# Nine chunks of a down projection as two-by-two blocks with seven products

## The chip, the cores and the metric

One core of a Trainium2 chip runs the kernel alone. The engines are TensorE (PE, whose weight loads the profile shows apart as PEld), VectorE (DVE), ScalarE (ACT), GpSimd (POOL) and SyncE (SP, which issues the transfers). The metric is the device time of one execution in microseconds; lower is better.

## The reference

Two layers, 256 tokens of 1024 features, all float32. Each layer is a half-step FFN, an attention mixer, and another half-step FFN. The change lies in the FFNs:

```python
def swiglu(h, w_gate, w_up, w_down):
    return (jax.nn.silu(h @ w_gate) * (h @ w_up)) @ w_down

for i in range(DEPTH):
    h = rmsnorm(x, ffn1_norm[i])
    x = x + 0.5 * swiglu(h, ffn1_w_gate[i], ffn1_w_up[i], ffn1_w_down[i])
    ...                         # the mixer adds to x
    h = rmsnorm(x, ffn2_norm[i])
    x = x + 0.5 * swiglu(h, ffn2_w_gate[i], ffn2_w_up[i], ffn2_w_down[i])
```

`w_gate` and `w_up` are 1024 x 2816, `w_down` is 2816 x 1024. The four FFNs are named here by (layer, which of the two): (0,1), (0,2), (1,1), (1,2).

## The kernel before

**Numbers in two parts.** TensorE multiplies in a reduced float32 form (F32R). Every operand is therefore held as `hi` (a cast of the float32 value, on ACT) and `lo` (value minus `hi`, on DVE), and each product is three matmuls: hi·hi, hi·lo and lo·hi. `dense` issues these three (lines L379, L382, L385), each with a stationary operand of 128 x 128 and 512 moving columns into one PSUM bank.

**Weights in chunks.** The weights pass through in chunks of 128 x 2048 floats (1 MB). `loader` issues a chunk's transfers on SP into one of three `raw` buffers (L270); `split_hi` casts it in four pieces of 512 columns on ACT (L300), `split_lo` subtracts in four pieces on DVE (L310). The pairs of hi and lo have four buffers (`NHL`). A chunk gives its pair back after its last use on TensorE, its `raw` buffer after its last `lo`.

**An FFN** has two stages. In the gate-and-up stage 11 groups of 256 hidden columns are computed, two chunks each, for two blocks `tb` of 128 tokens, into banks `gu`. `evac` forms h = silu(gate)·up (ACT `sil`, DVE `h`), turns it through DRAM (`hb`, `hd`, `hr`; transfers on SP) and splits it into `ht` (hi on ACT L515, lo on DVE L517). In the down stage 11 chunks of `w_down`, each two k-rows of 128 by two column halves `hf` of 512, are multiplied with `ht` into four banks `acc[tb][hf]`: 8 products, 24 matmuls a chunk. Chunks 0 to 7 go one after the other; the last three are the tail, in which the order is by (tb, hf) and then by chunk, so that one bank after the other is finished. `finish` then does x += 0.5·acc on DVE (L462), and `prep_half` transposes that half of x on TensorE (`xtp`, L392) and splits it for the next stage.

**What sets the order.** The program is laid out by a small planner (`Flow`): generators yield conditions or times, and an instruction is emitted when its modelled time has come. Each engine then runs its instructions in that order and waits on semaphores. The planner emits a split when a buffer pair is free in its model (`hl_left`), and, unless the chunk is due, only when its model of the engine is nearly free.

The chunks are numbered through the program: (0,2) has down chunks 73 to 83, (1,1) 106 to 116, (1,2) 153 to 163. So `lo79` is the lo part of down chunk 6 of (0,2).

Of the kernel before, what the change touches and what calls it, by code (L numbers as in the profile page):

```python
# [12 lines left out]
F32 = mybir.dt.float32  # L13
F32R = mybir.dt.float32r
# [28 lines left out]
SLACK = 0.4  # L43
AHEAD = 0
# [98 lines left out]
def kernel(  # L143
# [10 lines left out]
    nc = tc.nc  # L154
    PSUM = bass.MemoryType.PSUM
    NRAW, NHL, NT2 = 3, 4, 19
    flow = Flow()
# [3 lines left out]
    whl = ctx.enter_context(tc.tile_pool(name="whl", bufs=NHL))  # L161
# [15 lines left out]
    def bank(name, shape=(P, 4, P)):  # L177
        return banks.take(list(shape), F32, name)
# [61 lines left out]
    class Chunk:  # L240
        def __init__(self, parts):
            self.parts = parts
            self.raw = self.hi = self.lo = None
            self.arrive = self.early = None
            self.hit = [None] * 4
            self.lot = [None] * 4
            self.uses = 0

    chunks = []
    raw_left = [NRAW]  # L250
# [3 lines left out]
    at = [0]  # L254

    def add_chunk(parts, uses=8):
        c = Chunk(parts)
        c.uses = uses
        c.index = len(chunks)
        chunks.append(c)  # L260
        return c

    def loader():
        for i, c in enumerate(chunks):
            yield lambda: raw_left[0] > 0
            raw_left[0] -= 1
            c.raw = wraw.tile([P, 2048], F32, tag="raw", name=f"raw{i}")
            dma_free[0] = max(dma_free[0], flow.now)
            for j, (dst, src) in enumerate(c.parts):
                nc.sync.dma_start(out=dst(c.raw), in_=src)  # L270
                dma_free[0] += 2.9 / len(c.parts)
                if j == 1 and i < 2:
                    c.early = dma_free[0] + LAT
                    if i:
                        load_x(1, 1)
                        dma_free[0] += 0.7
            c.arrive = dma_free[0] + LAT
            if i == 0:
                load_x(1, 0)
                load_x(0, 1)  # L280
                dma_free[0] += 1.4
            if i > 4 and late_done[0] < len(late_loads):
                dst, src = late_loads[late_done[0]]
                late_done[0] += 1
                nc.sync.dma_start(out=dst, in_=src)
                dma_free[0] += 0.3

    def split_hi():
        for i, c in enumerate(chunks):
            yield lambda: c.raw is not None and hl_left[0] > 0  # L290
            hl_left[0] -= 1
            yield c.early or c.arrive
            c.hi = whl.tile([P, 2048], F32R, tag="hi", name=f"hi{i}")
            c.lo = whl.tile([P, 2048], F32R, tag="lo", name=f"lo{i}")
            for q in range(4):
                if q == 2:
                    yield c.arrive
                yield lambda: flow.free["A"] <= flow.now + SLACK or i <= at[0] + AHEAD
                sl = slice(q * 512, (q + 1) * 512)
                nc.scalar.copy(out=c.hi[:, sl], in_=c.raw[:, sl])  # L300
                c.hit[q] = flow.act(512)

    def split_lo():
        for i, c in enumerate(chunks):
            for q in range(4):
                yield lambda: c.hit[q] is not None
                yield c.hit[q]
                yield lambda: flow.free["V"] <= flow.now + SLACK or i <= at[0] + AHEAD
                sl = slice(q * 512, (q + 1) * 512)
                nc.vector.tensor_sub(c.lo[:, sl], c.raw[:, sl], c.hi.bitcast(F32)[:, sl])  # L310
                c.lot[q] = flow.dve(512)
            raw_left[0] += 1

    def k4(t):
        return t.rearrange("p (k n) -> p k n", k=4)
# [1 line left out]
    def k2(t):  # L317
        return t.rearrange("p (k n) -> p k n", k=2)
# [6 lines left out]

    def rows2(w, r):
        return [(lambda raw: k2(raw), w[r * 256:(r + 1) * 256, :].rearrange("(k p) n -> p k n", p=P))]

    def turned2(w, r):
        src = w[r * 256:(r + 1) * 256, :].rearrange("(k b i) n -> b i k n", k=2, b=4)  # L330
        return [((lambda raw, b=b: k2(raw)[b::4]), src[b]) for b in range(4)]
# [6 lines left out]
    def plan_ffn(l, nm, wg, wu, wd):  # L338
        gu = []
        for g in range(NG):  # L340
            ids = []
            for c in range(2):
                pieces = 2 if len(chunks) < 2 else 1
                a = cols4(wg[l], c, g * 256, 256, 0, pieces)
                b = cols4(wu[l], c, g * 256, 256, 256, pieces)
                ids.append(add_chunk([q for ab in zip(a, b) for q in ab]))
            gu.append(ids)
        plan[l, nm, "gu"] = gu
        dn = []
        for c in range(NG):  # L350
            dn.append(add_chunk(turned2(wd[l], c)))
        plan[l, nm, "dn"] = dn

    for l in range(DEPTH):
# [17 lines left out]
    def dense(ps, xh, xl, ready, c, need, sl, start, stop):  # L372

        flow.until(lambda: c.lot[need] is not None and ready() is not None)
        flow.at(ready())
        flow.at(c.lot[need])
        at[0] = max(at[0], c.index)
        wh, wl = sl(c.hi), sl(c.lo)
        nc.tensor.matmul(out=ps, lhsT=xh, rhs=wh, start=start, stop=False)  # L379
        flow.pe(T_MM)  # L380
        flow.step()
        nc.tensor.matmul(out=ps, lhsT=xh, rhs=wl, start=False, stop=False)  # L382
        flow.pe(T_MM)
        flow.step()
        nc.tensor.matmul(out=ps, lhsT=xl, rhs=wh, start=False, stop=stop)  # L385
        c.uses -= 1
        if c.uses == 0:
            hl_left[0] += 1
        return flow.pe(T_MM)

    def turn(dst, src, flipped=False):
# [82 lines left out]
    def ffn(l, nm, xt, gc_next):  # L474
        hts = [None] * NG
        htt = [None] * NG

        def evac(g, ps, end):
# [41 lines left out]
            hts[g], htt[g] = ht, t  # L520

        for g, ids in enumerate(plan[l, nm, "gu"]):
            flow.until(banks.has(2))
# [23 lines left out]

        SPLIT = NG - 3
        for c in range(SPLIT):
            for k in range(2):  # L550
                for tb in range(2):
                    for hf in range(2):
                        down(c, k, tb, hf)
            g4.give()
            if (l, nm) == (0, 1) and c == 2:
                flow.spawn(memory_prep())
# [814 lines left out]
```

## Time and profile before

| | |
|---|---|
| median of 3 runs | 970.88 us (970.84 to 972.41) |
| the profiled execution | 970.84 us, span from first to last instruction 969.1 us |
| TensorE matmuls | 960.4 us busy, 4552 instructions |
| VectorE | 681.8 us, 1428 instructions |
| ScalarE | 545.7 us, 1167 instructions |
| GpSimd | 60.2 us, 65 instructions |
| moved by transfers | 204.03 MB, 211 GB/s on average |

A share of busy time is a mean over all stages. What limits a stage is read from that stage: who waits there, and for whom. The durations of matmuls in the profile overlap, so their price is the distance from one start to the next.

### The profile page before, as it was taken

The numbers are of one execution on the slowest core, as the hardware profiler recorded it, in microseconds if no ns is written. First come the engines' busy times: TensorE is split into PE (matmuls) and PEld (weight loads), VectorE is DVE, ScalarE is ACT, GpSimd is POOL, SyncE is SP. The second block draws the span as 40 slices with busy tenths as digits, with TensorE's granted clock in tenths as the row PEclk, the third lists the DMA queues.
The fourth block names the chain that finished last, engine by engine and source line by source line (L and its number), as shares of the span: only waits on it lengthen the run. The fifth ranks groups of instructions, "written<-read, shape, count | busy, mean of one in ns | idle before, by whom it ended". The sixth has DMA issues, their size and how long they took to land.

```text
span 969.1 us, 13332 instructions
## 1 busy us (share of the span) xinstructions
PE 960.4 (99%) x4552; PEld 788.3 (81%) x4552; DVE 681.8 (70%) x1428; ACT 545.7 (56%) x1167; POOL 60.2 (6%) x65
## 2 busy tenths in 40 slices
PE   8999999999999999999999999999999999999998
PEld 7888888888777888888888888888787788888886
DVE  6777777788787877665566666654999986666641
ACT  6665555667675655554455545443677764545440
POOL 0000000021210000000000000000344100000000
PEclk9999999999999999999999999999999999999999
DMA  9988877385525587776648777764641468877741
GB/s 286 323 272 279 262 261 242 128 283 195 175 90 171 182 254 238 237 248 231 197 132 275 245 228 247 239 218 132 211 137 50 139 199 265 252 249 240 236 131 43
DMA packets 169295, 204.03 MB, mean 211 GB/s; under 512 B 9674, under 2 KB 144395, under 8 KB 169227
## 3 DMA queue, kind: packets, MB, share of 16 engines
q1 hardware_dynamic: 169226, 203.18, 65.3%
q8 instruction: 35, 0.57, 0.2%
q14 instruction: 34, 0.27, 0.1%
HBM read 188.99 MB, written 14.16 MB: 210 GB/s over the span
## 4 chain that ended last, share of the span: by engine, by line
PE 93%; DVE 4%; ACT 1%; DMA 1%; SPq 0%; issue 0%; ACTq 0%
PE gu L385 16%; PE gu L382 16%; PE gu L379 16%; PE acc L379 10%; PE acc L385 10%; PE acc L382 10%; PE pj L385 3%; PE pj L382 3%; PE pj L379 3%; DVE lo L310 1%; PE xtp L392 1%; PE S L1012 1%; PE AV L1093 1%; PE ptp L392 1%; PE kv L382 1%; PE kv L385 1%
## 5 line engine op out<-in xcount | busy, mean ns | idle before, releaser
L310 DVE TENSOR_TENSOR lo<-raw,hi 128x512 fp32r<-128x512 f32 x656 | 418.0, 684 | 196.2 <-ACT hi L300 182.6
L300 ACT CAST hi<-raw 128x512 fp32r<-128x512 f32 x656 | 367.0, 618 | 281.0 <-PE gu L385 149.9
L385 PE MATMUL gu<-hi,xl 128*128 128x512 f32 x704 | 274.3, 390 | 0.0
L379 PE MATMUL gu<-hi,xh 128*128 128x512 f32 x704 | 274.1, 389 | 0.0
L382 PE MATMUL gu<-lo,xh 128*128 128x512 f32 x704 | 274.0, 389 | 0.0
L382 PEld LDWEIGHTS gu<-lo,xh 128*128 128x128 f32 x704 | 132.2, 188 | 27.4
L385 PEld LDWEIGHTS gu<-hi,xl 128*128 128x128 f32 x704 | 132.2, 188 | 27.3
L379 PEld LDWEIGHTS gu<-hi,xh 128*128 128x128 f32 x704 | 132.2, 188 | 27.3
L379 PE MATMUL acc<-hi,ht 128*128 128x512 f32 x352 | 137.6, 391 | 0.0
L382 PE MATMUL acc<-lo,ht 128*128 128x512 f32 x352 | 137.2, 390 | 0.0
L385 PE MATMUL acc<-hi,ht 128*128 128x512 f32 x352 | 137.1, 390 | 0.0
L385 PEld LDWEIGHTS acc<-hi,ht 128*128 128x128 f32 x352 | 66.1, 188 | 13.7
L382 PEld LDWEIGHTS acc<-lo,ht 128*128 128x128 f32 x352 | 66.1, 188 | 13.5
L379 PEld LDWEIGHTS acc<-hi,ht 128*128 128x128 f32 x352 | 66.1, 188 | 13.5
L385 PE MATMUL pj<-hi,xl 128*128 128x512 f32 x160 | 64.5, 403 | 0.0
L382 PE MATMUL pj<-lo,xh 128*128 128x512 f32 x160 | 63.6, 397 | 0.0
L379 PE MATMUL pj<-hi,xh 128*128 128x512 f32 x160 | 63.5, 397 | 0.0
L487 ACT ACTIVATE sil<-gu,xr 128x256 f32<-128x256 f32 x88 | 41.4, 471 | 22.6 <-PE gu L385 22.6
L490 DVE SCALAR_TENSOR_TENSOR h<-gu,xr,sil 128x256 f32<-128x256 f32 x88 | 42.3, 480 | 2.3
L399 POOL TENSOR_TENSOR xr<-v,nhalf 128x1 f32<-128x1 f32 x12 | 8.4, 697 | 506.3 <-DVE v L397 506.3
L517 DVE TENSOR_TENSOR ht<-hr,ht 128x512 fp32r<-128x512 f32 x44 | 30.2, 686 | 13.4 <-ACT ht L515 12.9
L498 DVE STREAM_TRANSPOSE hb<-h 128x256 f32<-128x256 f32 x88 | 38.7, 440 | 1.1
(165 smaller groups left out, 828.0 us busy)
## 6 DMA issues: line engine op xcount, KB each, us to landing
raw<-in_ffn_w_down_dram SPq DMA_DIRECT2D x176, 256.0 KB, 4.1
raw<-in_ffn_w_gate_dram SPq DMA_DIRECT2D x86, 512.0 KB, 4.1
raw<-in_ffn_w_up_dram SPq DMA_DIRECT2D x86, 512.0 KB, 5.1
raw<-in_w_in_dram SPq DMA_DIRECT2D x32, 512.0 KB, 4.9
hd<-hb SPq DMA_DIRECT2D x44, 256.0 KB, 2.0
hr<-hd SPq DMA_DIRECT2D x44, 256.0 KB, 5.2
raw<-in_w_out_dram SPq DMA_DIRECT2D x8, 1024.0 KB, 4.9
raw<-in_w_mem_kv_dram SPq DMA_DIRECT2D x4, 1024.0 KB, 5.4
```

Of the source, the lines that this page charges most:

```text
L300: nc.scalar.copy(out=c.hi[:, sl], in_=c.raw[:, sl])
L310: nc.vector.tensor_sub(c.lo[:, sl], c.raw[:, sl], c.hi.bitcast(F32)[:, sl])
L379: nc.tensor.matmul(out=ps, lhsT=xh, rhs=wh, start=start, stop=False)
L382: nc.tensor.matmul(out=ps, lhsT=xh, rhs=wl, start=False, stop=False)
L385: nc.tensor.matmul(out=ps, lhsT=xl, rhs=wh, start=False, stop=stop)
L392: nc.tensor.transpose(out=dst, in_=src, identity=flip if flipped else ident)
L487: nc.scalar.activation(sil, ps[tb][:, 0:256], AF.Silu, scale=xt.r[tb])
L490: nc.vector.scalar_tensor_tensor(out=h, in0=ps[tb][:, 256:512], scalar=xt.r[tb], in1=sil, op0=ALU.mult, op1=ALU.mult)
L498: nc.vector.transpose(out=hb[:, :, tb].rearrange("p b f j -> p f b j"), in_=h.rearrange("p (f b i) -> p f b i", f=2, b=4))
L517: nc.vector.tensor_sub(lo, src, hi.bitcast(F32))
L1012: nc.tensor.matmul(out=ss[e][:, pr, :nk], lhsT=q[rows, pr, :], rhs=k[rows, pr, :], start=i == 0, stop=i == len(passes) - 1)
L1093: nc.tensor.matmul(out=av[64 * e:64 * e + 64, pr, :], lhsT=vsrc(kb, pr, e), rhs=pts[e][:, pr, kb, :], start=(kb == 0), stop=(kb == nb - 1))
```

## The change

In (0,2) and (1,1) down chunks 1, 4 and 6, and in (1,2) down chunks 1, 4 and 7, are computed as a product of two-by-two blocks. The blocks of h are (tb, k), those of the weights (k, hf). Seven block products take the place of eight (Strassen's scheme in Winograd's form):

- The weights need four sums of blocks (`wsum`, DVE, float32), and seven blocks are split into hi and lo where four were. Such a chunk takes two of the four buffer pairs.
- h needs four sums of its blocks (`sf`, 128 x 128 each, DVE); seven blocks of h are split (`h7`, in place of `ht`).
- Three of the seven products go into banks of `acc`. The other four are summed over the stage's three such chunks in four banks of their own (`m1`, `m5`, `m6`, `m7`).
- After the last of the three, `seven_sums` copies m1 to SBUF (ACT) and adds it and the other banks to x: four additions (L611) and four updates of x (L606) on DVE.

The core of the diff:

```diff
+    SEVEN = {(0, 1): (), (0, 2): (1, 4, 6), (1, 1): (1, 4, 6), (1, 2): (1, 4, 7)}
...
     def split_hi():
         for i, c in enumerate(chunks):
-            yield lambda: c.raw is not None and hl_left[0] > 0
-            hl_left[0] -= 1
+            n = 2 if c.seven else 1
+            yield lambda: c.raw is not None and hl_left[0] >= n
+            hl_left[0] -= n
...
     def split_lo():
         for i, c in enumerate(chunks):
-            for q in range(4):
+            if c.seven:
+                yield lambda: c.hi is not None and g2.left >= 6
+                yield c.arrive
+                r = [c.raw[:, q * 512:(q + 1) * 512] for q in range(4)]
+                t = [g2.take([P, 512], F32, "wsum") for _ in range(4)]
+                c.block = lambda q, r=r, t=t: ([r[0], r[2], r[3]] + t)[q]
+                for j, x, y in ((0, r[1], r[0]), (1, r[3], t[0]), (2, r[3], r[1]), (3, r[2], t[1])):
+                    yield calm_v(i)
+                    nc.vector.tensor_sub(t[j], x, y)
+                    c.tt[j] = flow.dve(512)
+            for q in range(7 if c.seven else 4):
...
+        def seven_forms(g, src):
+            yield lambda: g4.left >= 2 and g2.left >= 4 and (sv.index(g) < 2 or prog[0] >= sv[1])
+            ht = [g4.take([P, 8, P], F32R, "h7") for _ in range(2)]
+            sf = g2.take([P, 4, P], F32, "sf")
+            s1, s2, s3, s4 = (sf[:, j].rearrange("p (a j) -> p a j", a=4) for j in range(4))
+            for op, o, x, y in ((nc.vector.tensor_add, s1, src[:, 2], src[:, 3]), (nc.vector.tensor_sub, s2, s1, src[:, 0]),
+                                (nc.vector.tensor_sub, s3, src[:, 0], src[:, 2]), (nc.vector.tensor_sub, s4, src[:, 1], s2)):
+                op(o, x, y)
...
+        def seven(c, ms):
+            flow.until(lambda: hts[c] is not None)
+            ht, first, last = hts[c], c == sv[0], c == sv[-1]
+            for q, j, m in ((0, 0, 0), (1, 1, None), (2, 6, None), (3, 3, 1), (4, 4, 2), (5, 5, 3), (6, 2, None)):
+                ps = ms[m] if m is not None else acc.ps[q // 6][q // 2 % 2 if q < 6 else 0]
+                t = dense(ps, ht[0][:, j], ht[1][:, j], lambda: htt[c], dn[c], q, None,
+                          first and m is not None, last and m is not None)
...
+        def seven_sums(ms, t):
+            def into_x(tb, hf, v):
+                sl = slice(hf * 512, (hf + 1) * 512)
+                nc.vector.scalar_tensor_tensor(out=xs[tb][:, sl], in0=v, scalar=0.5, in1=xs[tb][:, sl],
+                                               op0=ALU.mult, op1=ALU.add)
...
+            nc.scalar.copy(out=u, in_=ms[0])
...
+            into_x(0, 0, u)
+            yield plus(u, u, ms[2])
+            plus(w, u, ms[1])
+            into_x(0, 1, w)
+            yield plus(u, u, ms[3])
+            into_x(1, 0, u)
+            yield plus(u, u, ms[1])
+            into_x(1, 1, u)
...
         for c in range(SPLIT):
+            prog[0] = c
+            if c in sv:
+                if c == sv[0]:
+                    flow.until(banks.has(4))
+                    ms = [bank(f"m{j}", (P, 512)) for j in (1, 5, 6, 7)]
+                t = seven(c, ms)
+                if c == sv[-1]:
+                    flow.spawn(seven_sums(ms, t))
+                continue
```

Two places where instructions move. First, VectorE ahead of the tail of (0,2). There, before, stand the lo's of chunks 9 and 10 (`lo82`, `lo83`), that of the next FFN's first chunk (`lo84`), and then x and its preparation:

```order
L310 TENSOR_TENSOR lo81_4683<-raw81_4590,hi81_4682 128x512 x4
L310 TENSOR_TENSOR lo82_4720<-raw82_4626,hi82_4719 128x512 x4
L310 TENSOR_TENSOR lo83_4757<-raw83_4665,hi83_4756 128x512 x4
L310 TENSOR_TENSOR lo84_4794<-raw84_4704,hi84_4793 128x512 x4
L462 SCALAR_TENSOR_TENSOR x0_85<-acc00_4463,x0_85 128x512
```

And now, from the same lo of chunk 9 to the third lo of chunk 10 (`msum` are the sums u and w, `m5` to `m7` the banks):

```order
L340 TENSOR_TENSOR lo82_0_4812<-raw82_4756,hi82_0_4811 128x512
L606 SCALAR_TENSOR_TENSOR x0_85<-msum_4818,x0_85 128x512
L611 TENSOR_TENSOR msum_4818<-msum_4818,m6_4544 128x512
L340 TENSOR_TENSOR lo82_0_4812<-raw82_4756,hi82_0_4811 128x512
L611 TENSOR_TENSOR msum_4819<-msum_4818,m5_4543 128x512
L606 SCALAR_TENSOR_TENSOR x0_85<-msum_4819,x0_85 128x512
L611 TENSOR_TENSOR msum_4818<-msum_4818,m7_4545 128x512
L340 TENSOR_TENSOR lo82_0_4812<-raw82_4756,hi82_0_4811 128x512
L606 SCALAR_TENSOR_TENSOR x1_86<-msum_4818,x1_86 128x512
L340 TENSOR_TENSOR lo82_0_4812<-raw82_4756,hi82_0_4811 128x512
L611 TENSOR_TENSOR msum_4818<-msum_4818,m5_4543 128x512
L340 TENSOR_TENSOR lo83_0_4843<-raw83_4797,hi83_0_4842 128x512
```

Behind these stand the last update of x from `msum`, three lo's of chunk 10, two of `lo84`, and x from `acc00`. The eight operations of `seven_sums` have come between the lo's of chunks 9 and 10.

Second, VectorE ahead of down chunk 6 of (0,2), whose lo's are `lo79`. Before:

```order
L310 TENSOR_TENSOR lo78_4563<-raw78_4437,hi78_4562 128x512 x2
L517 TENSOR_TENSOR ht_4569<-hr_4537,ht_4569 128x512
L310 TENSOR_TENSOR lo78_4563<-raw78_4437,hi78_4562 128x512 x2
L310 TENSOR_TENSOR lo79_4605<-raw79_4510,hi79_4604 128x512 x4
L310 TENSOR_TENSOR lo80_4644<-raw80_4545,hi80_4643 128x512 x4
```

And now (the rows named `sf` and `h7` are the forms of h for this chunk):

```order
L340 TENSOR_TENSOR lo78_0_4638<-raw78_4534,hi78_0_4637 128x512 x4
L573 TENSOR_TENSOR sf_4680<-hr_4157 128x128
L573 TENSOR_TENSOR sf_4680<-sf_4680,hr_4157 128x128
L573 TENSOR_TENSOR sf_4680<-hr_4157 128x128
L573 TENSOR_TENSOR sf_4680<-hr_4157,sf_4680 128x128
L586 TENSOR_TENSOR h7_4679<-hr_4157,h7_4678 128x256
L586 TENSOR_TENSOR h7_4679<-hr_4157,h7_4678 128x128
L586 TENSOR_TENSOR h7_4679<-sf_4680,h7_4678 128x512
L334 TENSOR_TENSOR wsum_4717<-raw79_4567 128x512
L334 TENSOR_TENSOR wsum_4718<-raw79_4567,wsum_4717 128x512
L334 TENSOR_TENSOR wsum_4719<-raw79_4567 128x512
L334 TENSOR_TENSOR wsum_4720<-raw79_4567,wsum_4718 128x512
```

Seven lo's of chunk 6 follow where four stood, and the last `ht` (that of chunk 10) has moved ahead, between the lo's of chunk 4.

More of the change, by code (lines that the diff above doesn't have):

```diff
@@ L244, in __init__, with part @@
             self.arrive = self.early = None
-            self.hit = [None] * 4
-            self.lot = [None] * 4
+            self.seven = False
+            self.hit = [None] * 7
+            self.lot = [None] * 7
+            self.tt = [None] * 4
             self.uses = 0
+        def part(self, lo, q):
+            t = (self.lo if lo else self.hi)
+            if self.seven:
+                t, q = t[q // 4], q % 4
+            return t[:, q * 512:(q + 1) * 512]
     chunks = []
@@ L267, in loader @@
             c.raw = wraw.tile([P, 2048], F32, tag="raw", name=f"raw{i}")
+            c.block = lambda q, c=c: c.raw[:, q * 512:(q + 1) * 512] if not c.seven else c.raw[:, (0, 2, 3)[q] * 512:
+                                                                                          (1, 3, 4)[q] * 512]
             dma_free[0] = max(dma_free[0], flow.now)
@@ L286, in loader, with calm_a, calm_v @@
                 dma_free[0] += 0.3
+    def calm_a(i):
+        return lambda: flow.free["A"] <= flow.now + SLACK or i <= at[0] + AHEAD
+    def calm_v(i):
+        return lambda: flow.free["V"] <= flow.now + SLACK or i <= at[0] + AHEAD
     def split_hi():
         for i, c in enumerate(chunks):
-            yield lambda: c.raw is not None and hl_left[0] > 0
-            hl_left[0] -= 1
+            n = 2 if c.seven else 1
+            yield lambda: c.raw is not None and hl_left[0] >= n
+            hl_left[0] -= n
             yield c.early or c.arrive
-            c.hi = whl.tile([P, 2048], F32R, tag="hi", name=f"hi{i}")
-            c.lo = whl.tile([P, 2048], F32R, tag="lo", name=f"lo{i}")
-            for q in range(4):
+            c.hi, c.lo = ([whl.tile([P, 2048], F32R, tag=x, name=f"{x}{i}_{j}") for j in range(n)] for x in ("hi", "lo"))
+            if not c.seven:
+                c.hi, c.lo = c.hi[0], c.lo[0]
+            for q in range(7 if c.seven else 4):
                 if q == 2:
                     yield c.arrive
-                yield lambda: flow.free["A"] <= flow.now + SLACK or i <= at[0] + AHEAD
-                sl = slice(q * 512, (q + 1) * 512)
-                nc.scalar.copy(out=c.hi[:, sl], in_=c.raw[:, sl])
+                if c.seven and q >= 3:
+                    yield lambda: c.tt[q - 3] is not None
+                    yield c.tt[q - 3]
+                yield calm_a(i)
+                nc.scalar.copy(out=c.part(0, q), in_=c.block(q))
                 c.hit[q] = flow.act(512)
@@ L304, in split_lo @@
         for i, c in enumerate(chunks):
-            for q in range(4):
+            if c.seven:
[8 more added lines that the diff above has]
+                    c.tt[j] = flow.dve(512)
+            for q in range(7 if c.seven else 4):
                 yield lambda: c.hit[q] is not None
                 yield c.hit[q]
-                yield lambda: flow.free["V"] <= flow.now + SLACK or i <= at[0] + AHEAD
-                sl = slice(q * 512, (q + 1) * 512)
-                nc.vector.tensor_sub(c.lo[:, sl], c.raw[:, sl], c.hi.bitcast(F32)[:, sl])
+                yield calm_v(i)
+                nc.vector.tensor_sub(c.part(1, q), c.block(q), c.part(0, q).bitcast(F32))
                 c.lot[q] = flow.dve(512)
-            raw_left[0] += 1
+                if q == 3:
+                    raw_left[0] += 1
+            if c.seven:
+                g2.give(4)
     def k4(t):
@@ L351, in plan_ffn @@
             dn.append(add_chunk(turned2(wd[l], c)))
+            if c in SEVEN[l, nm]:
+                dn[-1].seven, dn[-1].uses = True, 7
         plan[l, nm, "dn"] = dn
@@ L377, in dense @@
         at[0] = max(at[0], c.index)
-        wh, wl = sl(c.hi), sl(c.lo)
+        wh, wl = (c.part(0, need), c.part(1, need)) if sl is None else (sl(c.hi), sl(c.lo))
         nc.tensor.matmul(out=ps, lhsT=xh, rhs=wh, start=start, stop=False)
@@ L387, in dense @@
         if c.uses == 0:
-            hl_left[0] += 1
+            hl_left[0] += 2 if c.seven else 1
         return flow.pe(T_MM)
@@ L476, in ffn @@
         htt = [None] * NG
+        sv = SEVEN[l, nm]
+        prog = [-1]
         def evac(g, ps, end):
@@ L510, in evac @@
             yield flow.now + 4.0
+            src = hr.rearrange("p a (c j) -> p c a j", c=4)
+            if g in sv:
+                yield from seven_forms(g, src)
+                return
             yield g4.has()
             ht = g4.take([P, 2, 4, P], F32R, "ht")
-            src = hr.rearrange("p a (c j) -> p c a j", c=4)
             hi, lo = (ht[:, i].rearrange("p c (a j) -> p c a j", a=4) for i in range(2))
@@ L520, in evac @@
             hts[g], htt[g] = ht, t
+        def seven_forms(g, src):
[6 more added lines that the diff above has]
+                op(o, x, y)
+                t = flow.dve(P, 0.06)
+            yield t
+            view = lambda x: x.rearrange("p c (a j) -> p c a j", a=4)
+            parts = ((slice(0, 2), src[:, 0:2], view(ht[0][:, 0:2]), view(ht[1][:, 0:2])),
+                     (slice(2, 3), src[:, 3:4], view(ht[0][:, 2:3]), view(ht[1][:, 2:3])),
+                     (slice(3, 7), sf, ht[0][:, 3:7], ht[1][:, 3:7]))
+            ts = []
+            for js, x, hi, lo in parts:
+                nc.scalar.copy(out=hi, in_=x)
+                ts.append(flow.act(P * (js.stop - js.start)))
+            for (js, x, hi, lo), t in zip(parts, ts):
+                yield t
+                nc.vector.tensor_sub(lo, x, hi.bitcast(F32))
+                t = flow.dve(P * (js.stop - js.start))
+            g2.give(2)
+            hts[g], htt[g] = ht, t
@@ new lines, in seven @@
+        def seven(c, ms):
[5 more added lines that the diff above has]
+                          first and m is not None, last and m is not None)
+            g4.give(2)
+            return t
@@ new lines, in seven_sums, with plus @@
+        def seven_sums(ms, t):
[3 more added lines that the diff above has]
+                                               op0=ALU.mult, op1=ALU.add)
+                flow.dve(512)
+            def plus(o, v, m):
+                nc.vector.tensor_add(o, v, m)
+                return flow.dve(512)
+            yield t
+            yield g2.has(2)
+            u, w = (g2.take([P, 512], F32, "msum") for _ in range(2))
+            nc.scalar.copy(out=u, in_=ms[0])
+            yield flow.act(512)
+            banks.give()
+            calm = lambda: flow.free["V"] <= flow.now + SLACK
+            yield calm
+            into_x(0, 0, u)
+            yield calm
+            yield plus(u, u, ms[2])
+            banks.give()
+            yield calm
+            plus(w, u, ms[1])
+            into_x(0, 1, w)
+            yield calm
+            yield plus(u, u, ms[3])
+            banks.give()
+            yield calm
+            into_x(1, 0, u)
+            yield calm
+            yield plus(u, u, ms[1])
+            banks.give()
+            into_x(1, 1, u)
+            g2.give(2)
```

## The prediction

> **What bounds the kernel now.** I read the page first (engines, chain), then TensorE's waits, then the three down stages that the change touches, then single instructions in them. The page:
>
> ```profile
> span 969.1 us, 13332 instructions
> PE 960.4 (99%) x4552; PEld 788.3 (81%) x4552; DVE 681.8 (70%) x1428; ACT 545.7 (56%) x1167; POOL 60.2 (6%) x65
> PE 93%; DVE 4%; ACT 1%; DMA 1%; SPq 0%; issue 0%; ACTq 0%
> ```
>
> TensorE is the bound: 99% busy, 93% of the chain. Its waits in the whole run, longest first, begin with the start of the program and then fall to single waits of 0.4 us:
>
> ```profile
> PE xtp L392 <- DMA x<-in_x_dram: 1.6, 1, 1.6
> PE warm L1298 <- POOL ident masks.py:199: 1.3, 1, 1.3
> PE acc L379 <- DVE oT L1000: 0.4, 1, 0.4
> ```
>
> None is in a down stage of an FFN. The three down stages in question (layer 0 FFN 2, layer 1 FFN 1, layer 1 FFN 2), busy time by engine:
>
> ```profile
> 437.50:497.30 59.80, 59.80 (x271) 49.52 (x270) 30.54 (x51) 25.06 (x48) 0.55 (x1) 1.00 0.57 185
> 618.70:678.60 59.90, 59.90 (x271) 49.60 (x270) 30.37 (x51) 26.63 (x50) 0.55 (x1) 1.00 0.58 189
> 905.20:965.20 60.00, 60.00 (x265) 49.38 (x263) 24.08 (x39) 18.99 (x35) 0.00 (x0) 1.00 0.39 128
> ```
>
> PE is full, DVE half busy (behind the length and PE and PE's loads: 30.54 of 59.80 us), ACT 42%, the DMA engines 57%, the clock 1.00. So a matmul taken out here shortens the stage as long as the splits on ACT and DVE keep ahead. The price of a matmul is its distance to the next. First and last of the 264 in the last down stage:
>
> ```profile
> 905.21 0.39 PE L379 MATMUL acc<-hi,ht 128*128 128x512 f32 x1
> ...
> 964.82 0.39 PE L385 MATMUL acc<-hi,ht 128*128 128x512 f32 x1
> ```
>
> (964.82 − 905.21) / 263 = 0.2267 us (0.39 is a duration that overlaps its neighbours). A chunk of 24 takes 5.44 us. The Trainium skill (TensorE: Matmul & The Clock Gate, Part 1) gives 215.7 ns start to start at 512 columns; this trace has 226.7, and the trace decides; by the page the saving below would be an estimated 5.8 us.
>
> How the splits follow TensorE:
>
> ```profile
> 442.72 0.39 PE L385 MATMUL acc<-hi,ht 128*128 128x512 f32 x1
> 443.15 2.18 ACT L300 CAST hi<-raw 128x512 fp32r<-128x512 f32 x4 [2.38 <-PE acc L385]
> 443.80 2.50 DVE L310 TENSOR_TENSOR lo<-raw,hi 128x512 fp32r<-128x512 f32 x4 [1.62 <-ACT hi L300]
> 465.56 2.50 DVE L310 TENSOR_TENSOR lo<-raw,hi 128x512 fp32r<-128x512 f32 x4 [2.94 <-ACT hi L300]
> ```
>
> A chunk's last matmul slot ends at 442.95 (442.72 + 0.23); 0.20 us later ACT starts the hi casts into the freed buffer, and 0.65 us after that DVE starts the lo's. Four lo's last 2.50 us, so with 0.684 for one they start 0.605 apart; ACT's four last 2.18, so 0.52 apart. In every 5.44 us cycle DVE then idles 2.94. The chunk split here is read by PE three chunks (16 us) later: that lead, and those 2.94 us, are the cover for all new work.
>
> **The change part by part.** (Times in a stage from its start, 437.51, in layer 0 FFN 2.)
>
> *Removed matmuls.* A seven chunk has 7 block products of 3 matmuls, 21 for 24. Nine chunks: 27 × 0.2267 = 6.12 us, all on PE, the bound. Chunk starts move to c1 5.44, c2 10.20, c4 21.08, c5 25.84, c6 31.28, c7 36.04, the tail (chunks 8 to 10 together) 41.48, the end 57.80, instead of 59.84.
>
> *New splitting work.* Per seven chunk 4 subtractions (wsum) and 3 more lo's on DVE, 3 more hi's on ACT. Prices from these groups; the sums of m and x stand nearest to the three below them:
>
> ```profile
> L310 DVE TENSOR_TENSOR lo<-raw,hi 128x512 fp32r<-128x512 f32 x656 | 418.0, 684 | 196.2 <-ACT hi L300 182.6 <-DMA raw<-in_ffn_w_down_dram 7.6 <-DMA hr<-hd 3.8
> L300 ACT CAST hi<-raw 128x512 fp32r<-128x512 f32 x656 | 367.0, 618 | 281.0 <-PE gu L385 149.9 <-PE acc L385 87.9 <-issue 11.0
> L462 DVE SCALAR_TENSOR_TENSOR x<-acc,x 128x512 f32<-128x512 f32 x16 | 11.0, 690 | 21.7 <-PE acc L385 21.7
> L465 DVE TENSOR_TENSOR x<-acc,x 128x512 f32<-128x512 f32 x8 | 5.5, 688 | 1.8 <-PE acc L385 1.8
> L1026 ACT COPY PT<-ptp 128x512 f32<-128x512 f32 x17 | 9.8, 585 | 4.7 <-PE ptp L392 4.6
> L780 DVE TENSOR_TENSOR ropew<-ropew 128x64 f32<-128x64 f32 x20 | 4.4, 218 | 0.2
> L1101 DVE TENSOR_TENSOR oT<-AV,oT 128x256 fp32r<-128x256 f32 x10 | 4.2, 422 | 2.2 <-ACT oT L1099 1.9
> ```
>
> Per stage: 21 × 0.684 = 14.4 us on DVE; the sums are 4 adds and 4 updates of x, 8 × 0.69 = 5.5, and one 0.59 us copy on ACT.
>
> *Forms of h.* For one ht of 512 there are now four operations of 128 columns, not in this trace: between 0.22 (64 columns) and 0.42 (256), I take 0.29; and lo's of 256, 128 and 512: 4 × 0.29 + 0.42 + 0.29 + 0.68 = 2.55 us, 1.9 more than before. Two chunks' forms fall into the gate-and-up stage, where the lead hides them; the third falls into the down stage. DVE in the down stage: 30.5 + 14.4 + 5.5 + 2.5 = 52.9 of 57.8 us, so total room is there, but little; it must come in time.
>
> *The DVE queue against PE.* A seven chunk takes two of four buffer pairs, so splits start later relative to their use. Release plus 0.85, then 0.605 per 512-wide operation:
> - c3's lo's start at 5.44 + 0.85 = 6.29 and end 8.7; wsum of c4 to 11.1, its 7 lo's and an ht to 16.0. PE wants them at 21.08.
> - c5's lo's wait for c2's buffers (15.64): 16.5 to 18.9. Forms to 21.2, wsum of c6 23.6, its lo's 27.9; wanted at 31.28.
> - c7's lo's to 30.3 (wanted 36.04). Chunk 8's wait for c5's end (31.28): 32.1 to 34.6 (wanted 41.48).
> - Chunk 9 waits for the pair of c6's first four products (34.00): its first lo 34.9 to 35.5. Then the eight sums and seven lo's interleave, as in the change's list. The first sum finds m1 copied (ACT reaches that copy at about 35.2 and ends it at 35.8). Sums that wait for the operation just ahead start when it has ended, not 0.605 after it starts:
>
> ```profile
> 495.04 0.15 DVE L446 TENSOR_TENSOR sst<-xss 128x1 f32<-128x1 f32 x1
> 495.22 0.15 DVE L397 TENSOR_SCALAR v<-sst 128x1 f32<-128x1 f32 x1
> ```
>
> (0.03 us after the end), so 0.72. By that chunk 10's first lo is ready at 42.8 and its third at 44.6. PE wants the first after 12 matmuls of the tail and one more, 41.48 + 2.95 = 44.4, the third at 45.1. Margins 1.6 and 0.5 us: the third lo of chunk 10 is the tightest place.
> - After it x takes acc00, behind two lo's of the next stage, ending near 47.2; in PE's order the transposes that read it stand 27 matmuls into the tail, 47.6: margin 0.4. In layer 1 FFN 1 the same list and the same position.
> - Layer 1 FFN 2 has its last seven chunk just ahead of the tail (c7 ends at 41.48). Chunk 10's pair frees at 39.4; its third lo is done 1.8 us after c7, wanted at 3.6. The sums end long before PE does; the last x waits for acc as now.
>
> *Banks and transfers.* The four m banks were those of the last two gate-and-up groups; their h is read out by about 1.2 us into the stage, c1 starts at 5.44. DMA and SP:
>
> ```profile
> raw<-in_ffn_w_down_dram SPq DMA_DIRECT2D x176, 256.0 KB, 4.1
> hr<-hd SPq DMA_DIRECT2D x44, 256.0 KB, 5.2
> ```
>
> A raw buffer is free after the fourth lo. Chunk 10's load is issued when c7's lo's end (30.3), lands near 34.4, and its cast comes at 36.8. The last hr stands behind chunk 5's loads on SP, which wait for c2's lo's (about 5): ht at about 11, used in the tail. Cost nothing; the cover is 2.4 us at the nearest.
>
> *Sum.* −6.12, and for the two stages with small margins a lateness between 0 (PE cannot go faster than its spacing, so not below) and 1.3 us each (0.67 of the lo, as much of the transposes, from the first rival below); I take 0.3 each, near the lower end, because the four-lo rows run at 0.605 throughout the down stage: −5.5. The profiled execution is 970.84 us, 1.74 outside its span, and the median of the runs 970.88: span 963.6, time 965.3.
>
> **Rivals.**
> 1. *DVE works at its full durations.* From c3's first lo (6.29) to chunk 10's third are 54 operations of 512 columns and one set of forms: 54 × 0.684 + 2.55 = 39.5, ready at 45.78 against 45.11: 0.67 late, and the transposes as much again, in two stages: gain 6.1 − 2.7 = 3.4, time 967.4. For it: wsum and sums depend on each other. Against: the 2.50 us rows; only some nine of the 54 wait for the operation directly ahead. The Trainium skill (VectorE: DVE Perf Modes, The DRAIN you can't avoid) says the next DVE instruction does not start until the pipe is empty. By that rule this rival is the forecast; the trace's four lo's disagree with it (2.50, not 2.74), its dependent pair agrees.
> 2. *DVE becomes the bound: slower.* The same count at a price p per operation is late by 54 p + 2.55 + 6.29 − 45.1 = 54 p − 36.3 per stage. Two stages eat all 6.12 us from p = 0.73 on; at 0.75, 2 × 4.2 = 8.4 lost, time 973.1. It needs nearly every operation to wait for the last one's end, plus reads of banks slower than L465 shows.
> 3. *Buffers come free later than I read it*, only at the end of a whole seven chunk: chunks 9 and 10 then start to split at 36.04 + 0.85, 2.0 us later, of which margins take 0.5: about 1.5 lost in two stages, 0.5 in the third: gain 2.6, time 968.2, at the edge of no change.
> 4. *It doesn't do what it says:* the 189 remaining products' matmuls run farther apart (changing banks, new buffers). To eat 6.12 us they need 0.032 us each; against it, every third matmul changes banks now too, at 0.2267.
>
> **How the numbers follow.** No change is within 0.2% (1.9 us), about what a measurement of this kernel tells apart. Forecast 965.3: 0.70. Rival 1: 0.13. Rival 3: 0.06, half of it counted as the same. Rival 4: 0.05, same. Rival 2: 0.06, slower. Faster 0.86, same 0.08, slower 0.06. The range starts at all of 6.12 saved, less 0.4 for the spread of runs, 964.3, and takes in rival 1: up to 967.8.
>
> **What the next profile would show.** Right: 27 fewer matmuls with the same 0.227 spacing, down stages near 57.8 to 58.4 us, DVE at 51 to 53 us in the first two, no PE wait over 0.5 us there. A PE wait at the third block of chunk 10, or at xtp, says rival 1 or 3; many waits from c4 on, and DVE without gaps, rival 2; a wider matmul spacing, rival 4. I am wrong if the 0.605 spacing does not hold for wsum, whose inputs are fp32 throughout, or for adds that read a bank.

## The result, and the profile after

| | before | after |
|---|---|---|
| median, same chip | 970.91 us (970.84 to 972.41) | 965.56 us (964.95 to 967.37) |
| profiled execution | 970.84 us, span 969.1 | 964.95 us, span 963.2 |
| matmuls | 4552 | 4525 |

The ratio is 0.9943, 95% interval 0.9930 to 0.9955: faster by 5.5 us. The forecast was 965.3 us (964.3 to 967.8).

The page of the changed kernel, engines and chain:

```profile
span 963.2 us, 13464 instructions
PE 954.8 (99%) x4525; PEld 783.9 (81%) x4525; DVE 745.0 (77%) x1569; ACT 567.9 (59%) x1215; POOL 60.5 (6%) x65
PE 94%; DVE 3%; ACT 1%; DMA 1%; SPq 0%; issue 0%; ACTq 0%
```

27 matmuls are gone, VectorE has 63 us more work and ScalarE 22, and TensorE is still 99% busy. TensorE's longest waits:

```profile
PE warm L1425 <- POOL ident masks.py:199: 1.4, 1, 1.4
PE xtp L429 <- DMA x<-in_x_dram: 1.1, 2, 0.9
PE ptp L429 <- DVE pe L1266: 0.7, 2, 0.6
PE acc L416 <- DVE oT L1127: 0.4, 1, 0.4
```

As before, none lies in a down stage. The three changed stages by engine (length; PE, PE's loads, DVE, ACT, POOL; clock, DMA share, GB/s):

```profile
437.60:495.50 57.90, 57.90 (x263) 47.94 (x262) 49.77 (x88) 31.74 (x62) 0.55 (x1) 1.00 0.65 209
616.80:674.80 58.00, 58.00 (x263) 48.01 (x263) 49.72 (x88) 33.04 (x63) 0.55 (x1) 1.00 0.65 209
901.30:959.20 57.90, 57.90 (x256) 47.72 (x255) 43.63 (x76) 25.78 (x49) 0.00 (x0) 1.00 0.47 150
```

These windows are cut to the forecast length of a stage; the first two stages run some 1.5 us past them, because transposes stand among the tail's matmuls. VectorE went from 30.5 to 49.8 us of a stage, and TensorE has no gap. First matmul of layer 0 FFN 2's down stage and first of the next stage, then first and last of the last down stage:

```profile
437.67 0.39 PE L416 MATMUL acc<-hi,ht 128*128 128x512 f32 x1
496.92 0.39 PE L416 MATMUL gu<-hi,xh 128*128 128x512 f32 x1
901.37 0.39 PE L416 MATMUL acc<-hi,ht 128*128 128x512 f32 x1
958.94 0.39 PE L422 MATMUL acc<-hi,ht 128*128 128x512 f32 x1
```

496.92 − 437.67 = 59.25 us, where it was 61.29. Layer 1 FFN 1, from its first matmul to its last, takes 59.02 us where it was 61.07, and the last stage 57.57 where it was 59.61. Each lost 2.04 us, together 6.12: nine chunks of three matmuls at 0.2267, with nothing given back. The span fell by 5.9; the 0.2 between are the start (0.16 later) and a 0.08 longer way between stages.

The tightest place, VectorE ahead of the tail of layer 0 FFN 2 (start, duration, group; a row with x5 is five instructions):

```profile
473.52 0.69 DVE L606 SCALAR_TENSOR_TENSOR x<-msum,x 128x512 f32<-128x512 f32 x1 [0.31 <-ACT msum L617]
474.32 0.69 DVE L611 TENSOR_TENSOR msum<-msum,m 128x512 f32<-128x512 f32 x1
...
479.85 0.68 DVE L340 TENSOR_TENSOR lo<-raw,hi 128x512 fp32r<-128x512 f32 x1
480.45 0.69 DVE L606 SCALAR_TENSOR_TENSOR x<-msum,x 128x512 f32<-128x512 f32 x1
481.05 3.09 DVE L340 TENSOR_TENSOR lo<-raw,hi 128x512 fp32r<-128x512 f32 x5
484.07 0.68 DVE L499 SCALAR_TENSOR_TENSOR x<-acc,x 128x512 f32<-128x512 f32 x1
```

and TensorE's matmul that reads the third lo of chunk 10, and the transposes that read x:

```profile
482.77 0.39 PE L419 MATMUL acc<-lo,ht 128*128 128x512 f32 x1
485.27 0.60 PE L429 MATMUL xtp<-ident,x 128*128 128x128 f32 x4
```

Chunk 10's lo's are the row at 479.85 and the first three of the row at 481.05. The third starts at 481.65 and ends at 482.33, 44.66 us into the stage (44.6 was worked out); TensorE reads it at 482.77, 0.44 later. x ends at 484.75, 0.52 before its transposes. In layer 1 FFN 1 the same two margins are 0.43 and 0.52. These margins of half a microsecond carry the result.

### The profile page after: what moved, and what is told of

The parts are those of the page before. It is cut to its first block, busy times and chain, and to the rows that moved or that the text cites. A ratio compares the mean times of both kernels' runs of the same rounds, so it can differ in the third digit from the quotient of the medians.

```text
span 963.2 us, 13464 instructions
## 1 busy us (share of the span) xinstructions
PE 954.8 (99%) x4525; PEld 783.9 (81%) x4525; DVE 745.0 (77%) x1569; ACT 567.9 (59%) x1215; POOL 60.5 (6%) x65
## 4 chain that ended last, share of the span: by engine, by line
PE 94%; DVE 3%; ACT 1%; DMA 1%; SPq 0%; issue 0%; ACTq 0%
PE gu L422 17%; PE gu L416 17%; PE gu L419 17%; PE acc L416 9%; PE acc L422 9%; PE acc L419 9%; PE pj L422 3%; PE pj L416 3%; PE pj L419 3%; PE xtp L429 1%; PE ptp L429 1%; PE S L1139 1%; PE AV L1220 1%; PE m L422 1%; PE m L419 1%; PE m L416 1%
## 5 line engine op out<-in xcount | busy, mean ns | idle before, releaser
L340 DVE TENSOR_TENSOR lo<-raw,hi 128x512 fp32r<-128x512 f32 x647 | 413.7, 684 | 103.9 <-ACT hi L321 100.0
L321 ACT CAST hi<-raw 128x512 fp32r<-128x512 f32 x647 | 361.7, 618 | 219.0 <-PE gu L422 123.6
L419 PE MATMUL gu<-lo,xh 128*128 128x512 f32 x704 | 274.0, 389 | 0.0
L419 PEld LDWEIGHTS gu<-lo,xh 128*128 128x128 f32 x704 | 132.2, 188 | 27.3
L416 PE MATMUL acc<-hi,ht 128*128 128x512 f32 x280 | 109.6, 391 | 0.0
L422 PE MATMUL acc<-hi,ht 128*128 128x512 f32 x280 | 109.2, 390 | 0.0
L419 PE MATMUL acc<-lo,ht 128*128 128x512 f32 x280 | 109.1, 390 | 0.0
L419 PE MATMUL pj<-lo,xh 128*128 128x512 f32 x160 | 63.6, 397 | 0.0
L422 PEld LDWEIGHTS acc<-hi,ht 128*128 128x128 f32 x280 | 52.6, 188 | 11.0
L419 PEld LDWEIGHTS acc<-lo,ht 128*128 128x128 f32 x280 | 52.6, 188 | 10.7
L416 PEld LDWEIGHTS acc<-hi,ht 128*128 128x128 f32 x280 | 52.6, 188 | 10.7
L559 DVE TENSOR_TENSOR ht<-hr,ht 128x512 fp32r<-128x512 f32 x35 | 24.1, 687 | 32.2 <-ACT ht L557 32.2
L557 ACT CAST ht<-hr 128x512 fp32r<-128x512 f32 x35 | 21.6, 618 | 41.9 <-DMA hr<-hd 41.8
```

The lines of the kernel that those rows point to most:

```text
L321: nc.scalar.copy(out=c.part(0, q), in_=c.block(q))
L340: nc.vector.tensor_sub(c.part(1, q), c.block(q), c.part(0, q).bitcast(F32))
```

## The experiments

All were run in several rounds beside the kernel before on one chip per group; ratios are to that. Medians of before in the three groups were 971.17, 971.59 and 972.46 us, so the ratio is the number to read, and stage lengths are read from traces. To compare in microseconds, a ratio is multiplied by 970.9.

### Is the new work hidden? Do each half of the change alone

e1: the kernel before, with one of the eight block products of the nine chunks left out (27 matmuls fewer, none of the new work).

```diff
+                        if c in drop and (k, tb, hf) == (1, 1, 0):
+                            continue
```

> The kernel before, with one of the eight products left out in the same nine chunks and none of the new work (its output lacks those products). My theory: all of the change's new work is hidden, so this saves the same 27 matmuls and nothing more: span 969.1 - 6.1 = 963.0, time 964.8, within 0.3 us of the changed kernel. Rival (part of the saving was lost again to late splits or transposes): this kernel is faster than the changed one by that loss, 0.6 us or more.

e2: the change with an eighth product, so the new work without the saving.

```diff
-                dn[-1].seven, dn[-1].uses = True, 7
+                dn[-1].seven, dn[-1].uses = True, 8
...
+            t = dense(acc.ps[1][1], ht[0][:, 2], ht[1][:, 2], lambda: htt[c], dn[c], 6, None, False, False)
```

> The changed kernel with an eighth product in each of the nine chunks (the seventh once more, into the fourth bank of acc, so the output is not the reference's). All the new work stays, the saving goes. My theory: the time of the kernel before, 970.9, within 0.4. Rival (VectorE's new work costs time by itself): slower than before, by 1 us or more.

Measured: e1 965.87 us, ratio 0.9934 (0.9921 to 0.9947), against the change's 0.9943 (0.9930 to 0.9955); e2 971.68, ratio 0.9998 (0.9987 to 1.0008). By the ratios alone e1 is 0.9 us ahead of the change, which is within their intervals and so doesn't settle the rival of 0.6 us or more. The stage lengths do: e1's are 59.25, 59.03 and 57.57 us, the change's 59.25, 59.02 and 57.57; e2's are 61.29, 61.06 and 59.61, those of before to 0.01. VectorE has 30.7 us of work in e1's first stage and 49.8 in the change's, and the saving is the same; the work alone moves nothing. In these stages what TensorE is spared is the whole effect, and the added work is hidden.

### How large is the margin? Four more additions

e3: behind the first update of x from `msum`, four more additions into `w`, whose result nobody reads.

```diff
             into_x(0, 0, u)
+            for _ in range(4):
+                nc.vector.tensor_add(w, u, u)
```

> The changed kernel with four more additions of 512 columns on VectorE among the sums of each of the three stages, each waiting for the one ahead (0.72 us). My theory: the lead is nearly used up at one place, the third lo of chunk 10 (0.45 us left in the trace), so the four (2.9 us) show at once: 2.4 us in each of two stages, 2.9 - 1.8 = 1.1 in the third, together +6, time about 971; with a spacing of 0.605 it would be +4.5, time 969.5. Rival (VectorE is idle for 8 us of each stage, so 3 us more are hidden): no more than 0.5 us over the changed kernel.

Measured: 973.11 us, ratio 1.0013 (1.0000 to 1.0027), 0.7% or 6.8 us above the change: its whole gain is gone. TensorE's waits in the trace, and the two at chunk 10 of layer 0 FFN 2, then of layer 1 FFN 1:

```profile
PE acc L419 <- DVE lo L340: 5.1, 5, 1.2
```

```profile
483.60 0.50 PE L419 MATMUL acc<-lo,ht 128*128 128x512 f32 x1 [1.12 <-DVE lo L340]
...
485.40 0.72 PE L419 MATMUL acc<-lo,ht 128*128 128x512 f32 x1 [0.83 <-DVE lo L340]
485.93 0.63 PE L422 MATMUL acc<-hi,ht 128*128 128x512 f32 x1
486.35 0.63 PE L416 MATMUL acc<-hi,ht 128*128 128x512 f32 x1
```

```profile
667.11 0.50 PE L419 MATMUL acc<-lo,ht 128*128 128x512 f32 x1 [1.12 <-DVE lo L340]
...
668.92 0.50 PE L419 MATMUL acc<-lo,ht 128*128 128x512 f32 x1 [0.84 <-DVE lo L340]
669.25 0.39 PE L422 MATMUL acc<-hi,ht 128*128 128x512 f32 x1
669.49 0.39 PE L416 MATMUL acc<-hi,ht 128*128 128x512 f32 x1
```

So 8 us of idle VectorE in a stage is no room: 2.9 us of work at the wrong place in its row comes out on TensorE. The stages grew by 4.11, 2.55 and 1.49 us, 8.15 in all (span 971.6 against 963.2). The expectation was 2.4, 2.4 and 1.1: the second stage agrees, the third lost 0.4 more. The first two have the same waits, and differ by 1.56 us: in the first, the matmuls behind the second wait stand some 0.427 us apart (485.93 to 486.35) instead of 0.227, eight of them. The granted clock (the column ahead of the last two) in the window of those waits, in the one behind it, and in the window of the waits of layer 1 FFN 1 (why these edges, the last section says):

```profile
482.10:485.51 3.41, 1.46 (x6) 0.59 (x4) 3.41 (x7) 0.53 (x2) 0.00 (x0) 1.00 0.56 183
485.51:488.92 3.41, 3.41 (x9) 2.64 (x10) 3.41 (x6) 0.00 (x0) 0.00 (x0) 0.50 0.84 276
666.42:669.83 3.41, 1.88 (x7) 1.27 (x8) 3.41 (x7) 0.00 (x0) 0.00 (x0) 1.00 0.83 258
```

### The sums at another place

e7: the third seven chunk is chunk 7 in all three stages. e10: the same, with the four additions.

```diff
-    SEVEN = {(0, 1): (), (0, 2): (1, 4, 6), (1, 1): (1, 4, 6), (1, 2): (1, 4, 7)}
+    SEVEN = {(0, 1): (), (0, 2): (1, 4, 7), (1, 1): (1, 4, 7), (1, 2): (1, 4, 7)}
```

> The changed kernel with the third seven chunk of all three stages at chunk 7, just ahead of the tail, where it was chunk 6 in two of them. My theory, by the same count of VectorE's queue: chunk 10's lo's then stand ahead of most sums (1.8 us of room for the third), x from acc00 ends 1.1 us before its transposes: no lateness, the time of the changed kernel (965.0 to 965.6). Rival (the sums beside the tail hold back x and its transposes, the reason to keep them apart): 1.3 us or more slower in each of two stages, 967.5 or more.

> The third seven chunk at c=7 in all three stages, and the same four dummy additions behind the first update of x from msum. Computes the same output. Theory (each operation costs its place in VectorE's row, and only what ends after TensorE wants it is late): with c=7 two lo's of chunk 10 stand ahead of the sums, so the four dummies (4 x 0.72 = 2.9 us) push only the third and fourth. Without dummies the third lo ends at 481.07 and TensorE wants it at about 482.6, a margin of 1.5; so about 1.4 us late in each of three stages, and x from acc00 some 2 to 2.9 us later than 483.9 with little margin of its own: the loss is 1.4 to 2.9 us a stage, 4 to 8.5 in all, time 970 to 974.5; the wait in the trace stands at the third lo of chunk 10 (L419), no more than 1.6 us long, and at xtp. Compared with the same dummies at c=6 (2 stages paid about 3.4 each), a stage pays less per dummy on lo and the rest on xtp. Rival (VectorE's idle time in the stage, some 8 us, takes them anywhere): 966, no wait. Rival (any operation added to VectorE ahead of the tail is paid in full, 2.9 us a stage): 974.7.

Measured: e7 966.03 us, ratio 0.9943 (0.9928 to 0.9958); e10 974.51, ratio 1.0034 (1.0022 to 1.0046). By its ratio e7 gains as much as the change, but not without a wait: 0.6 us at L419 in layer 1 FFN 1, where the first lo of chunk 10 stands behind two sums and the others behind four; that stage is 0.9 us longer. In e10 the stages are 1.44, 5.22 and 1.45 us longer than the change's. The 1.4 read off layer 0 FFN 2 held there and in the last stage; in layer 1 FFN 1 two waits of 1.50 and 1.57 and the low clock behind them followed. The time, 974.2 by the ratio, is near the upper end of what was expected (974.5), because the margin had been read in one stage and taken for three. The rival that every operation is paid in full (974.7) gives this time too; the stage lengths speak against it, 1.44 and 1.45 where it has 2.9.

### More seven chunks, and where they break

e5: three seven chunks in layer 0 FFN 1 as well. e9: chunks 1, 4 and 7 in all four FFNs. e6: chunks 1, 3, 5 and 7 in the three stages of the change.

```diff
-    SEVEN = {(0, 1): (), (0, 2): (1, 4, 6), (1, 1): (1, 4, 6), (1, 2): (1, 4, 7)}
+    SEVEN = {(0, 1): (1, 4, 6), (0, 2): (1, 4, 6), (1, 1): (1, 4, 6), (1, 2): (1, 4, 7)}      # e5
+    SEVEN = {(0, 1): (1, 4, 7), (0, 2): (1, 4, 7), (1, 1): (1, 4, 7), (1, 2): (1, 4, 7)}      # e9
+    SEVEN = {(0, 1): (), (0, 2): (1, 3, 5, 7), (1, 1): (1, 3, 5, 7), (1, 2): (1, 3, 5, 7)}    # e6
```

> The change plus down chunks 1, 4 and 6 of layer 0 FFN 1. Computes the same output. There VectorE was busy 49 of 60 us already, with the memory's preparation (32 meml of 0.34 us, ropew) among it; 22.4 us more make 71 of 57.8. In the row the splits go first and meml moves behind the sums, into the mixer. Removed: 36 matmuls, 8.16 us. Theory (place and due time decide): what moves behind (meml, 8.9 us) is wanted by kv from about the tail's last part on; some of it comes late, an estimated 2 us, about what the nine matmuls save: 965.5 (963.5 to 967.5), waits at kv or at xtp near the end of that stage, none in the other three. Rival (all hidden): 963.5. Rival (VectorE's time over the stage's length is paid in full, 71 - 58 = 13 us): 975 or more.

> Seven chunks at c = 1, 4 and 7 in all four FFNs, twelve in all. Computes the same output. Theory: as the run with layer 0 FFN 1 at 1, 4, 6, but the sums stand at the tail's start and fewer meml are pushed behind them, and the other two stages have a margin of 1.5 us where 0.4 was: 965 (963 to 967), at or up to 1 us below that run. Rival (the last place of the sums delays x and the transposes when VectorE is full): 967 or more, with waits at xtp.

> Four seven chunks (c = 1, 3, 5, 7) in each of the three stages, twelve in all. Computes the same output. Matmuls removed: 36 x 0.2267 = 8.16 us. Theory (the place in VectorE's row decides): the splits keep ahead up to the tail; in the tail the first lo of chunk 10 stands behind two sums and the next three behind four, so the third ends about 4.6 us after the tail starts and is wanted at 3.6: late 0.8 to 1.0 in each of three stages. Gain 8.16 - 2.7 = 5.5, time 965.4 (964.5 to 966.5), a wait of about 0.9 at L419 in each stage. Rival (VectorE's busy time decides): 49.8 + 7 x 0.684 + 2.5 = 57.1 of the 57.1 us stage: full, so every wait for a cast lands on TensorE, 8 us of them as now: late by several us a stage, time 972 or more. Rival (all new work stays hidden): 963.0.

Measured: e5 979.97 us, ratio 1.0089 (1.0076 to 1.0102); e9 976.01, ratio 1.0042 (1.0027 to 1.0057); e6 984.48, ratio 1.0130 (1.0117 to 1.0143). All three miss, by 14, 10 and 18 us. In e5 the other stages kept the change's lengths; the down stage of layer 0 FFN 1 came out 9.1 us longer than with its saving of 2.04, and the way from there to the next FFN's down stage 6.7 longer. In e9 the same two came out 5.5 and 6.8 us longer, with waits for lo's and for `meml` as in e5 and not at xtp, where its rival had them, and layer 1 FFN 1 was 0.9 us longer as in e7. TensorE's waits in e5, and VectorE's row ahead of the longest:

```profile
PE acc L419 <- DVE lo L340: 6.0, 3, 2.7
PE kv L422 <- DVE meml L789: 2.4, 3, 0.9
```

```profile
181.15 0.62 DVE L789 SCALAR_TENSOR_TENSOR meml<-mr,gcol,memh 128x128 fp32r<-128x128 f32 x2 [1.81 <-ACT memh L785]
181.68 3.09 DVE L340 TENSOR_TENSOR lo<-raw,hi 128x512 fp32r<-128x512 f32 x5
```

I had priced what moves behind (`meml`) but not walked that stage's row up to the tail, where the lo's came up to 2.7 us late. I had also read the 49 of 60 us from a stretch (154 to 214 us) that is not this stage (130.5 to 191.5, VectorE 44.9 of 61.3 us). The time is that of the rival (VectorE's time over the stage's length is paid in full), but VectorE was not full: 60.8 of 68.05 us. Ahead of TensorE's longest wait two `meml` stood ahead of chunk 10's lo's and waited 1.81 us for ScalarE, so place had a part here too; how large a part, no run shows. In e6 the row of layer 0 FFN 2 shows what I had not walked either:

```profile
446.20 0.68 DVE L340 TENSOR_TENSOR lo<-raw,hi 128x512 fp32r<-128x512 f32 x1
451.58 0.69 DVE L559 TENSOR_TENSOR ht<-hr,ht 128x512 fp32r<-128x512 f32 x1 [4.69 <-ACT ht L557]
452.19 1.29 DVE L340 TENSOR_TENSOR lo<-raw,hi 128x512 fp32r<-128x512 f32 x2
```

The last `ht`, which only the tail needs, stood ahead of chunk 3's lo's and waited for h's return: VectorE was idle for 4.69 us with work behind it. From 451.6 to 483.2 it then worked 31.4 of 31.6 us, and TensorE waited in each stage, nine times and 13.1 us in all, here three times:

```profile
460.68 0.50 PE L419 MATMUL acc<-lo,ht 128*128 128x512 f32 x1 [1.23 <-DVE lo L340]
...
485.73 0.50 PE L419 MATMUL acc<-lo,ht 128*128 128x512 f32 x1 [1.64 <-DVE lo L340]
...
488.26 0.50 PE L419 MATMUL acc<-lo,ht 128*128 128x512 f32 x1 [1.55 <-DVE lo L340]
```

### Is it the amount of work, or its place?

e15: e6 with that `ht` emitted later. e16: also the sums, but the first update of x, behind chunk 10's lo's. Both do all of e6's work.

```diff
+            if g == NG - 1 and sv:
+                yield lambda: prog[0] >= 4
             yield g4.has()
...
             into_x(0, 0, u)
+            yield lambda: dn[NG - 1].lot[3] is not None        # e16 only
             yield calm
```

> Four seven chunks a stage (1, 3, 5, 7) as in the run before, with one edit: the ht of the stage's last group is emitted only when the program has reached down chunk 4, so that it no longer stands ahead of chunk 3's lo's. Computes the same output. Theory (a waiting instruction at the head of VectorE's row did the damage: 4.69 us idle behind that ht at 446.9 to 451.6, and from there VectorE had no gap left): without it the splits of chunks 4 to 9 end ahead of their use again, and only the third lo of chunk 10, behind four of the sums, is late, by about 1.0 us in each of three stages. Gain 8.16 - 3.0 = 5.2, time 965.8 (964.5 to 967.5), no waits at L419 outside the tail. Rival (VectorE's busy time, 57 of 57 us, is the limit, wherever the work stands): still 980 or more, with waits from chunk 4 on. Rival (half the damage is the clock after the waits): in between, 970 to 976.

> As that, and all sums but the first update of x are emitted only behind the four lo's of chunk 10. Computes the same output. Theory (place decides): the third lo of chunk 10 ends 2.6 us after the tail's start and is wanted at 3.6; x from acc00 ends near 45.8 us into the stage and the transposes want it at 46.9. So nothing is late: 36 x 0.2267 = 8.16 us saved, 2.04 more than the change, time 963.3 (962.6 to 964.5), no wait in the down stages. Rival (VectorE's busy time): 975 or more. Rival (the sums pushed back make x late for the transposes): waits of 0.5 to 1.2 us at xtp, time 965 to 967.

Measured: e15 967.43 us, ratio 0.9954 (0.9942 to 0.9967); e16 963.83, ratio 0.9911 (0.9898 to 0.9924). The first edit took back 17 of the 18 us that e6 was behind the change, the second 4 more, with VectorE busier than ever and TensorE full (e16, layer 1 FFN 1):

```profile
616.80:674.80 58.00, 58.00 (x264) 48.03 (x263) 55.01 (x99) 35.83 (x69) 0.00 (x0) 1.00 0.63 205
```

So in these stages the place of the work decides, up to 55 of 58 us. The clock, the last rival for e6, was the smaller part: e6 has two slow windows, with some 1.6 us lost in each. Against the expectations: e15's waits at L419 are 3.6 us in three places, up to 1.6 long where 1.0 was expected. e16 saved its 0.68 us more a stage in full in layer 1, but not in layer 0 FFN 2:

```profile
484.42 0.69 DVE L340 TENSOR_TENSOR lo<-raw,hi 128x512 fp32r<-128x512 f32 x1 [1.69 <-ACT hi L321]
485.03 0.68 DVE L499 SCALAR_TENSOR_TENSOR x<-acc,x 128x512 f32<-128x512 f32 x1
```

```profile
485.77 0.66 PE L429 MATMUL xtp<-ident,x 128*128 128x128 f32 x4 [1.30 <-DVE x L499]
```

A lo of the next stage waits for its cast at the head of the row, x from acc00 stands behind it, and the transposes wait 1.30 us: the same pattern once more. e16 is the fastest kernel here: 0.9% faster than before, and its interval ends below the change's. How far ahead of the change it is stays open: by the ratios 3 us, by the spans of the two traces 1.1 (962.1 and 963.2), by the three stages 0.6 (0.7 less in each of two, 0.8 more in layer 0 FFN 2).

## Why the prediction was right

- **What bounds it.** TensorE, in these stages without a wait, before and after. 27 × 0.2267 = 6.12 us came out as 3 × 2.04.
- **Lateness.** Taken as 0.3 us in each of two stages, measured 0, the lower bound. Of the 0.6 us too many, 0.2 went into the start and the way between stages, which were not in the sum: span 963.2 for 963.6. The median (965.56) is 0.6 above the profiled execution, where they agreed before; so the forecast of 965.3 stands 0.3 below it. That it came so near is in part luck: the lateness that did not come about and the median's distance from the profiled execution cancel.
- **Stage lengths.** 57.8 to 58.4 us were to be seen. The last stage has 57.57 to the start of its last matmul, the first two 59.02: the sum for their ends left out the transposes among the tail's matmuls. They were there before too (61.07), so the saving is untouched.
- **The ledger of VectorE's row.** Chunk 10's first lo was to end at 42.8 us and the third at 44.6; measured 42.86 and 44.66. So the 0.605 us spacing also holds for wsum and for sums that read banks; operations that need the one just ahead start about 0.72 after it (0.80 for the first addition, which overwrites what the update ahead of it reads).
- **Prices.** wsum 0.68 us, sums 0.68 to 0.69 (0.69 taken), the copy of m1 0.577 (0.59), 128 columns 0.28 to 0.29 (0.29), 256 columns 0.395 (0.42). VectorE had 49.8 us a stage, not 51 to 53: its idle time shrank less than the sum of durations suggests, since durations overlap in a row.
- **Rival 1 (full durations; 967.4)** and **rival 2 (VectorE becomes the bound)** did not come about, but e3 shows how near they were: 2.9 us of VectorE's time in the row is all that lay between the change and no gain. The Trainium skill (VectorE: DVE Perf Modes, The DRAIN you can't avoid) says that the next operation starts only when the pipe is empty, and adds that one that is not held starts earlier; rival 1 took the first half alone. In the trace the independent operations do start earlier (rows below).
- **Rival 3 (buffers only at a chunk's end)**: no: chunk 9's first lo started 34.85 us into the stage, where 34.9 was worked out and 2.0 more would have been this rival's. **Rival 4 (wider spacing)**: no; the spacing is 0.2267 still, in e2, with all 216 matmuls of the nine chunks back, the time is that of before (0.9998).

## What to carry to other kernels

Work moved from a full engine to a half-empty one is free only where it stands early enough in that engine's row: walk the row, instruction by instruction, in every stage it is put into, to the time at which the full engine reads the result. The share of idle time says nothing about it; 2.9 us at a bad place cost the whole gain, part of it by the clock that fell behind the waits, and 55 of 58 us at good places cost nothing. First look for an instruction that waits at the head of the row with work behind it that others need sooner, and put it later.

## What the runs showed of the hardware

**Short waits add up within windows of 3.41 us, and TensorE's clock follows.** In the traces of all twelve kernels the recorded changes of the granted clock lie whole steps of 3.413 us apart: in e3 the change at 485.51 is 140.0 steps behind the first one (7.64), in e6 those at 488.70 and 963.16 are 141.0 and 280.0 behind 7.42. Between two such edges TensorE's idle time counts as a sum. In e3's layer 0 FFN 2 both waits fall into one window, busy for 1.46 of 3.41 us and so idle for 1.95 (rows above): the next window runs at half the clock, with eight matmuls some 0.427 us apart, 1.56 us lost beside the waits. In layer 1 FFN 1 an edge at 666.42 cuts the same pair of waits; 0.44 us of idle time fall ahead of it, 1.53 behind, and the clock stays up.

Over all traces, by the busy times of the profile, nine windows at full clock were followed by a slow one while the program ran on. They were idle for 1.69 and 2.31 us (e9), 1.72 and 2.45 (e5), 1.82 (e10), 1.95 (e3), 1.99 and 2.11 (e6), and 2.03 (e2, near its start). No other window at full clock was idle for longer than 1.62 us but one, at e1's start, with 1.70. So in these runs the limit lies near 1.7 us, half a window. Each slow window without idle time was followed by full clock; the four slow ones with 0.85 us of it or more were followed by another slow one.

The Trainium skill (TensorE: Matmul & The Clock Gate, HAM oscillation — how this bites in real kernels) warns of idle gaps over about 3.4 us. No wait in a down stage here was longer than 2.7 us, and the clock fell all the same; the traces decide.

**VectorE's overlap depends on the operands.** The first three sums of h's blocks and the first two weight sums:

```profile
457.15 0.28 DVE L573 TENSOR_TENSOR sf<-hr 128x128 f32<-128x128 f32 x1
457.46 0.29 DVE L573 TENSOR_TENSOR sf<-sf,hr 128x128 f32<-128x128 f32 x1
457.68 0.28 DVE L573 TENSOR_TENSOR sf<-hr 128x128 f32<-128x128 f32 x1
...
459.45 0.68 DVE L334 TENSOR_TENSOR wsum<-raw 128x512 f32<-128x512 f32 x1
460.17 0.69 DVE L334 TENSOR_TENSOR wsum<-raw,wsum 128x512 f32<-128x512 f32 x1
460.78 0.68 DVE L334 TENSOR_TENSOR wsum<-raw 128x512 f32<-128x512 f32 x1
```

An operation that reads the result just ahead starts 0.03 to 0.04 us after its end (457.46; 460.17); one that doesn't starts some 0.07 us before that end (457.68; 460.78). Writing what the one just ahead writes holds an operation too: e3's four additions all write w and read only u, and last 2.87 us together, so they start 0.73 us apart.
